# A streaming encoder step on one core: the last quarter of the second feed-forward product as seven products, GpSimd's key parts in pieces, an early sigmoid

## The chip, the cores and the metric

The kernel runs on one core of one Trainium2 chip. A core has a matrix engine (TensorE, PE in the profile, with its weight loads as PEld), VectorE (DVE), ScalarE (ACT), GpSimd (POOL) and SyncE (SP), which here only issues DMAs. The engines work side by side and wait for each other through semaphores; each runs its own instructions in a fixed order. The metric is the device time of one launch in microseconds (us), as the median of several runs.

## The reference, cut to what matters

All tensors are fp32. 576 frames (512 of the prompt, 64 of the sample) go through one layer; the change touches what stands behind the two attentions.

```python
x = LN1(alpha * x + mix @ W_o)
hid = square(relu(x @ W_up))              # 1024 -> 4096
x = LN2(alpha * x + hid @ W_down)         # 4096 -> 1024
gate = sigmoid(x @ W_ple_gate + b_ple_gate)
y = x + gate * (p @ W_ple)
```

Both layer norms subtract the mean, divide by the square root of the variance plus an epsilon, and apply a gain and an offset.

## The kernel before, in words

**Layout.** Activations lie with features across the 128 partitions and the 576 tokens along the free axis. `Y` [128, 8, 576] is the residual. `A` and `B` are the token halves 0 to 287 and 288 to 575; the last stages of the kernel before use `A2` (0 to 255) and `B2` (256 to 575) instead. PE instructions keep a 128x128 weight and stream the tokens.

**A product in fp32.** Both operands are split into a high part and a low remainder, and three matmuls (high by high, high by low, low by high) are summed in PSUM (`gemm`, line 308; `quad`, line 296, does the first piece of the gate product in another order). For the weights, ACT rounds a loaded tile `wraw` to the high half of `whl` (L149), and DVE subtracts it to give the low half (L158). For the activations, `BH` and `BL` are the high and low parts behind a layer norm (L1249 by ACT, L1253 by DVE), `hidE`/`hidO` and `hA` to `hD` those of hidden columns.

**Seven products.** Most of the feed-forward work multiplies 2x2 blocks with seven block products instead of eight (`seven`, `up_pair`, `down_pair`); sums of weight blocks and of operands make up for it. Of a unit of weights, `add_seven` loads one block sum by an ordinary load and a second load that adds to it on the way (an accumulating DMA, issued by POOL, L213), and two more sums are made by DVE in place (L184, L187). The hidden columns come in eight groups of 512; groups 6 and 7, the last quarter of W_down, are done plainly by `down_last`: 192 matmuls of 256 columns for A2, then 192 of 320 for B2.

**The tail.** `LayerNorm` is written as a generator, stepped by the loop of matmuls that it runs beside (`drive`): sum over features (`add`), mean by a matmul with `onesm` (L1200), subtract, square on ACT, sum, variance (`var`, L1220), a square root on ACT (L1222), a reciprocal on DVE (L1223), a transpose by PE that spreads it (L56), then in four parts: a product on DVE (L1236), gain and offset on ACT (L1247), high part on ACT (L1249), low part on DVE (L1253). LN2 of A2 runs under `down_last(B2)`, and LN2 of B2 under the gate product of A2 (192 matmuls of 256 columns). The gate product of B2 (192 of 320) closes the kernel, with sigmoid, product and sum by ACT and DVE, and the store. `PL` is p @ W_ple, written to HBM early (`PLD`) and loaded again by one DMA of 2304 KB (L1699) for the end.

**What sets the order.** A list scheduler works from the program order with priorities (`tc.high_priority`); matmuls of `seven` are held to program order. Weight tiles go through small rings of buffers, so a load is issued when its buffer is free, and loads of one queue land in order. ACT holds one table of functions at a time: an `ACT_TABLE_LOAD` goes ahead of the first function from another one. `early` is a square root of a constant, placed ahead of LN1 so that the table is there in time (L1662).

## Time and profile before

| what | value |
|---|---|
| median of 3 runs | 764.45 us (764.35 to 764.53) |
| the profiled execution, its own time | 764.96 us |
| its span in the trace | 763.2 us |
| PE busy | 751.1 us (98% of the span), 5679 matmuls |
| DVE busy | 570.3 us (75%) |
| ACT busy | 472.6 us (62%) |
| POOL busy | 118.0 us (15%) |
| the chain that ended last | PE 78%, DVE 13%, ACT 7% |

The span is the trace's length from the first to the last instruction; some 1.8 us of the execution's own time lie around it. Busy shares are means over the whole span, so a stage is read from a view of its own stretch. A time of the chain or the timeline counts from the start of the span.

### The profile page before, as it was taken

How to read it: one execution, taken by the hardware profiler on the slowest of the kernel's cores; microseconds unless marked ns; L12 is line 12 of the kernel's file. 1: busy time of each engine (PE TensorE's matmuls, PEld its weight loads, DVE VectorE, ACT ScalarE, POOL GpSimd, SP SyncE). 2: the span in 40 equal slices, each digit the busy share in tenths (PEclk: the TensorE clock that was granted, in tenths of full speed). 3: DMA queues.
4: the chain of work that ended last, by engine and by line, in shares of the span. 5: the costliest groups of instructions: out<-in, count | busy, mean ns of one | idle time of the engine just before them, and what ended most of it. 6: DMA issues, size and time to landing. Idle time of an engine off the chain costs nothing.

```text
span 763.2 us, 14659 instructions
## 1 busy us (share of the span) xinstructions
PE 751.1 (98%) x5679; PEld 731.1 (96%) x5679; DVE 570.3 (75%) x1119; ACT 472.6 (62%) x931; POOL 118.0 (15%) x162
## 2 busy tenths in 40 slices
PE   9999999999999999999999999999999999999997
PEld 7999998999999999999999999999999999999997
DVE  6788888888777766779787589866897766757643
ACT  6589777888667535788643577435763466525351
POOL 7100434445341000100000000000000000011000
PEclk9999999999999999999999999999999999999999
DMA  8538344254223325352447667667657564730001
GB/s 286 169 69 151 128 131 127 71 174 161 82 94 92 97 74 168 125 160 84 112 111 188 157 143 178 148 156 189 160 134 186 159 144 147 287 116 28 28 29 69
DMA packets 38198, 101.35 MB, mean 133 GB/s; under 512 B 6000, under 2 KB 10224, under 8 KB 38000
## 3 DMA queue, kind: packets, MB, share of 16 engines
q1 hardware_dynamic: 34384, 87.61, 37.4%
q0 software_dynamic: 3456, 12.58, 10.1%
q8 instruction: 44, 0.72, 0.4%
q10 hardware_dynamic: 288, 0.22, 0.1%
q14 instruction: 26, 0.21, 0.1%
HBM read 85.26 MB, written 9.54 MB: 124 GB/s over the span
## 4 chain that ended last, share of the span: by engine, by line
PE 78%; DVE 13%; ACT 7%; issue 2%; DVEq 0%; ACTq 0%
PE g L308 39%; PE m L308 14%; PE n L308 13%; PE g L296 2%; DVE dbias L713 2%; PE T L56 2%; ACT xr L791 2%; DVE whl L158 2%; DVE m L711 1%; PE V L978 1%; ACT whl L149 1%; PE m L472 1%; DVE sP L911 1%; PE m L486 1%; PE S L903 1%
## 5 line engine op out<-in xcount | busy, mean ns | idle before, releaser
L149 ACT CAST whl<-wraw 128x1024 fp32r<-128x1024 f32 (+2 forms) x190 | 154.9, 828 | 83.8 <-PE g L308 49.8
L158 DVE TENSOR_TENSOR whl<-wraw,whl 128x1024 fp32r<-128x1024 f32 (+2 forms) x158 | 157.9, 1009 | 54.0 <-ACT whl L149 53.4
L308 PE MATMUL m<-AH,whl 128*128 128x288 f32 x736 | 176.6, 307 | 0.0
L308 PE MATMUL g<-BH,whl 128*128 128x288 f32 (+2 forms) x680 | 143.3, 298 | 0.0
L308 PEld LDWEIGHTS m<-AH,whl 128*128 128x128 f32 x736 | 126.4, 188 | 1.7 <-issue 1.0
L308 PEld LDWEIGHTS g<-BH,whl 128*128 128x128 f32 x680 | 111.1, 188 | 1.3
L308 PE MATMUL m<-AL,whl 128*128 128x288 f32 x368 | 108.7, 295 | 0.0
L308 PE MATMUL g<-BL,whl 128*128 128x288 f32 (+2 forms) x340 | 100.6, 296 | 0.3 <-DVE BL L1253 0.3
L308 PEld LDWEIGHTS m<-AL,whl 128*128 128x128 f32 x368 | 69.5, 189 | 0.7
L213 POOL DMA_DIRECT2D wraw<-in_w_dram x24 | 20.7, 864 | 287.2 <-DMA wraw<-in_w_dram 173.3
L308 PEld LDWEIGHTS g<-BL,whl 128*128 128x128 f32 x340 | 64.0, 188 | 0.9 <-DVE BL L1253 0.7
L158 POOL TENSOR_TENSOR whl<-wraw,whl 128x256 fp32r<-128x256 f32 x64 | 50.6, 821 | 84.2 <-ACT whl L149 70.0
L916 ACT ACTIVATE sP<-sP,st 128x128 f32<-128x128 f32 (+4 forms) x72 | 39.5, 550 | 36.1 <-DVE st L911 36.0
L308 PE MATMUL m<-BH,whl 128*128 128x288 f32 x192 | 42.9, 302 | 0.0
L308 PE MATMUL g<-s,whl 128*128 128x288 f32 x288 | 42.1, 295 | 0.0
L308 PE MATMUL n<-BH,whl 128*128 128x288 f32 x192 | 42.0, 294 | 0.0
L308 PEld LDWEIGHTS g<-s,whl 128*128 128x128 f32 x288 | 39.5, 188 | 0.0
L308 PEld LDWEIGHTS m<-BH,whl 128*128 128x128 f32 x192 | 32.0, 188 | 0.5 <-issue 0.3
L56 PE MATMUL T<-ident,sP 128*128 128x128 f32 (+1 forms) x176 | 31.1, 273 | 1.0 <-DVE sP L925 0.6
L308 PEld LDWEIGHTS n<-BH,whl 128*128 128x128 f32 x192 | 32.0, 188 | 0.0
L1523 ACT ACTIVATE g<-n 128x288 f32<-128x288 f32 x24 | 9.5, 395 | 35.6 <-PE n L308 35.6
L308 PE MATMUL m<-BL,whl 128*128 128x288 f32 x96 | 28.3, 294 | 0.0
(331 smaller groups left out, 1662.1 us busy)
## 6 DMA issues: line engine op xcount, KB each, us to landing
wraw<-in_w_dram SPq DMA_DIRECT2D x48, 512.0 KB, 4.0
wraw<-in_w_dram POOLq DMA_DIRECT2D x24, 512.0 KB, 5.7
wraw<-in_w_qkv_dram SPq DMA_DIRECT2D x23, 512.0 KB, 4.0
wraw<-in_w_dram SPq DMA_DIRECT2D x24, 256.0 KB, 4.2
wraw<-in_w_up_dram SPq DMA_DIRECT2D x8, 512.0 KB, 4.0
wraw<-in_w_down_dram SPq DMA_DIRECT2D x8, 512.0 KB, 4.5
wraw<-in_w_gate_dram SPq DMA_DIRECT2D x8, 512.0 KB, 4.6
wraw<-in_w_o_dram SPq DMA_DIRECT2D x8, 384.0 KB, 3.1
```

The lines of the kernel that those rows point to most:

```text
L56: PE.transpose(out, in_, ident[:n, :n])
L149: ACT.copy(self.hv[u][:, 0, c], src["tile"][:, c])
L158: eng.tensor_tensor(t[:, 1, p], src["tile"][:, p], f(t[:, 0, p]), OP.subtract)
L213: POOL.dma_start(t[:, :n], it["acc"], accum_op=OP.add)
L296: PE.matmul(ps, W(w, k, slice(0, 128)), a[:, k, sl], start=(len(terms) == 2 and n == 0), stop=False)
L308: mm = PE.matmul(ps, W(w, kw, wc), a[:, ka, cols], start=(first and i == 0), stop=(last and i == n - 1), skip_group_check=more)
L472: PE.matmul(mk[:, h, :HW], w0(part, k), a[:, k, h * HW:(h + 1) * HW], start=(k == 0 and i == 0), stop=(k == 7 and i == 2))
L486: PE.matmul(acc[b][:n[b], :304], a[:, k, b * 128:b * 128 + n[b]], ixw(part, k), start=(k == 0 and i == 0), stop=(k == 7 and i == 2))
L713: tc.keep_in_program_order(DVE.match_replace(out=s, in_to_replace=m, in_values=s, imm_value=GONE))
L791: q(lambda r=r, s=s: ACT.mul(v2(xr[r * 32:r * 32 + 32]), v[s * 32:s * 32 + 32], sc))
L916: ACT.activation(j["P"], j["P"], AF.Exp, bias=j["st"][:, 0:1], scale=-1.0, accum_out=j["st"][:, 2:3])
L1523: ACT.mul(P.e, P.o, -1.0)
```

## The change

The last quarter of W_down is done in seven block products as well. Their order is not that of `seven`: `five(L2B)` does the five products that need the weight sums, for all four pairs of output columns (240 matmuls of 288 columns; new units of weights, `add_five`), and completes half B of the residual; then `two()` does the remaining two products for half A with plain W_down (96 matmuls of 288). LN2 of B runs beside `two()`, LN2 of A beside the gate product of B. Both gate products are now of 288 columns. Matmuls of these last stages: 768 before, 720 now.

Beside it: the sums of a layer norm built with `soon` are made on DVE and not on POOL (L1A, L2B); the layer norms of the tail take their buffers from those of finished products (`Carved`); PL is loaded ahead of `five`; GpSimd's subtractions for the keys (`KL`) are made in two pieces each; `early` has a buffer of its own, and a sigmoid of a constant is issued right behind the square root of L2A; the last column is split 176/112 instead of 192/128.

```diff
+        def add_five(self, ap):
+            u = len(self.cs)
+            self.cs += [128] * 3
+            r1 = self.source(ap[:, 0:1024], acc=ap[:, 1024:2048])
+            r2 = self.source(ap[:, 2048:3072])
+            lo, hi, all2 = slice(0, 512), slice(512, 1024), slice(0, 1024)
+            def t1():
+                DVE.tensor_tensor(r2["tile"][:, lo], r2["tile"][:, lo], r1["tile"][:, lo], OP.add)
+            def t2():
+                DVE.tensor_tensor(r2["tile"][:, hi], r2["tile"][:, hi], r2["tile"][:, lo], OP.add)
+            self.split(u, r2, [lo], DVE)
+            self.split(u + 1, r1, [all2], DVE)
+            self.piece(u + 1, None, t1, r1, r2)
+            self.piece(u + 2, None, t2, r2)
+            self.split(u + 2, r2, [all2], DVE)
+            return u
...
-        for kind, n in (("P", 4 if q else 0), ("Q", 4 if q < 3 else 0)):
+        for kind, n in (("P", 4 if q else 0), ("Q", 4)):
             for x in range(n):
-                U[kind, q, x] = WT.add_seven(I["w_7"][n7])
+                U[kind, q, x] = (WT.add_five if (kind, q) == ("Q", 3) else WT.add_seven)(I["w_7"][n7])
                 n7 += 1
-    for g in range(G_DOWN, NG):
-        for c in range(4):
-            U["D", g, c] = WT.add(I["w_down"][(g - G_DOWN) * 4 + c], 256, whole=True)
+    for c in range(4):
+        U["D", c] = WT.add(I["w_down"][c], 256, whole=True)
...
-        q(lambda: eng.tensor_tensor(KL[lo, 0], k32[lo, :NP], f(QE[lo, :NP]), OP.subtract))
-        q(lambda: eng.tensor_tensor(KL[hi, 1], k32[hi, :NP], f(QO[hi, :NP]), OP.subtract))
+        cuts = (slice(0, 256), slice(256, NP)) if eng is POOL else (slice(0, NP),)
+        for r, x, t in ((lo, 0, QE), (hi, 1, QO)):
+            q(lambda r=r, x=x, t=t: [eng.tensor_tensor(KL[r, x, c], k32[r, c], f(t[r, c]), OP.subtract) for c in cuts])
...
+            self.soon, self.scaling = soon, False
+            self.eng = DVE if soon else POOL
...
-                (DVE if self.sl is A else POOL).tensor_tensor(self.s, y[:, 0:2], y[:, 2:4], OP.add)
+                self.eng.tensor_tensor(self.s, y[:, 0:2], y[:, 2:4], OP.add)
-                (DVE if j == 6 or self.sl is A else POOL).tensor_tensor(self.s, self.s, y[:, j:j + 2], OP.add)
+                (DVE if j == 6 else self.eng).tensor_tensor(self.s, self.s, y[:, j:j + 2], OP.add)
...
+            first = tc.high_priority if self.soon else ExitStack
...
-            ACT.activation(rt[:, :m], var[:, :m], AF.Sqrt, bias=epst[:, 0:1])
+            root = ACT.activation(rt[:, :m], var[:, :m], AF.Sqrt, bias=epst[:, 0:1])
+            if gi and sl is A:
+                with tc.issue_after(root.ins), tc.high_priority():
+                    ACT.activation(early[:, 0:1], epst, AF.Sigmoid, bias=epst[:, 0:1])
...
-        split("12", v)
-        later(2, lambda: tt(v, v, F[0], OP.add))
+        d = 6 if g == NG - 1 else 0
+        split("12", v, d)
+        later(2 + d, lambda: tt(v, v, F[0], OP.add))
         if g > 1:
-            split("s4", v, 2)
...
+    def five(ln):
+        tt = DVE.tensor_tensor
+        oldest = [U["Q", 3, 0]]
+        def product(u, n, ps, first=True):
+            while owed.get(ROWS[n]):
+                pop_now()
+            x = HX[ROWS[n]]
+            W = WT.quarter(u, n, oldest[0])
+            for _ in gemm(ps, W, range(4), x[0], x[1], slice(0, HW), first=first, more=not first, pin=True):
+                WT.step()
+                yield 1
+        os = {}
+        def start(c):
+            u = U["Q", 3, c]
+            o = psum_n()[:, :HW]
+            yield from product(u, "11", o)
+            os[c] = d = psM.tile([128, 2, 512], F32, name="g", tag="m", bufs=2)[:, 1, :HW]
+            with tc.high_priority():
+                ACT.copy(d, o)
+            y = Y[:, 2 * c, A]
+            later(0, lambda: tt(y, y, o, OP.add))
+        yield from start(0)
+        for c in range(4):
+            u = U["Q", 3, c]
+            y0, y1 = Y[:, 2 * c], Y[:, 2 * c + 1]
+            oldest[0] = u + 1
+            z = psB.tile([128, 2, 512], F32, name="g", tag="g", bufs=1)[:, 0, :HW]
+            yield from product(u, "t0", z)
+            later(0, lambda z=z, y0=y0: tt(y0[:, B], y0[:, B], z, OP.add))
+            later(0, lambda z=z, y1=y1: tt(y1[:, B], y1[:, B], z, OP.subtract))
+            if c < 3:
+                yield from start(c + 1)
+            d = os[c]
+            yield from product(u, "t1", d, False)
+            r = fs.tile([128, 2, 2, HW], F32, name="r", bufs=2)[:, 0, 0]
+            with tc.high_priority():
+                ACT.mul(r, d, -1.0)
+            e = psum_n()[:, :HW]
+            yield from product(u, "t3", e)
+            oldest[0] = u + 2
+            def both_halves(r=r, y1=y1):
+                y = y1.rearrange("p (a t) -> p a t", a=2)
+                tt(y, y, r[:, None, :].to_broadcast([128, 2, HW]), OP.add)
+            later(0, lambda r=r, e=e: tt(r, r, e, OP.add))
+            later(0, both_halves)
+            yield from product(u, "t2", d, False)
+            def last(d=d, y0=y0, c=c):
+                with tc.high_priority():
+                    tt(y0[:, B], y0[:, B], d, OP.add)
+                    ln.add(2 * c)
+            later(0, last)
+    def two():
+        def prepare(c):
+            m = psum_g()
+            ACT.copy(m[:, :, :HW], Y[:, 2 * c:2 * c + 2, A])
+            return m
+        nxt = prepare(0)
+        for c in range(4):
+            W = unit_w(U["D", c])
+            m = nxt
+            if c < 3:
+                nxt = prepare(c + 1)
+            for x, n in ((0, "12"), (1, "s4")):
+                for _ in gemm(m[:, x, :HW], W, range(4), HX[n][0], HX[n][1], slice(0, HW),
+                              wc=slice(x * 128, (x + 1) * 128), first=False, more=True):
+                    WT.step()
                     yield 1
+            later(0, lambda c=c, m=m: ACT.copy(Y[:, 2 * c:2 * c + 2, A], m[:, :, :HW]))
...
-    L1A = LayerNorm(A, 0, (4, 5, 2, 12))
-    L1B = LayerNorm(B, 0, (3, 8, 7, 12))
+    L1A = LayerNorm(A, 0, (4, 5, 2), True)
+    L1B = LayerNorm(B, 0, (3, 8, 7))
     L1 = both(L1A, L1B)
     drive(wo2(A, L1A, 3), 8, None, 0)
-    early = lnp[0].tile([128, 4], F32, name="ln_r", bufs=2)
+    early = base.tile([128, 1], F32, name="early")
     ACT.activation(early[:, 0:1], epst, AF.Sqrt, bias=epst[:, 0:1])
...
-        if g < G_DOWN:
+        if g < NG - 2:
             todo += [down_pair(g + 1, c) for c in range(4)]
     drive(seven(todo), len(todo) * 14, None, 0)
+    PL = base.tile([128, 8, NT], F32, name="PL", tag="AH")
+    SP.dma_start(PL.rearrange("p j t -> p (j t)"), PLD)
+    lnp[0] = Carved()
+    L2B = LayerNorm(B, 2, (5, 9, 3), True)
+    L2A = LayerNorm(A, 2, (5, 8, 2))
+    drive(five(L2B), 40, None, 0)
     WT.lag = 1
+    drive(two(), 16, iter(L2B), 32, False)
+    while not L2B.scaling:
+        L2B.pump()
     pS.close()
     fe = ctx.enter_context(tc.tile_pool(name="fe", bufs=1))
     WT.ring(fe, 0, 5, "e")
     lnp[0] = fe
-    PL = base.tile([128, 8, NT], F32, name="PL", tag="AH")
-    SP.dma_start(PL.rearrange("p j t -> p (j t)"), PLD)
-    L2A = LayerNorm(A2, 2, (4, 8, 2, 0))
-    L2B = LayerNorm(B2, 2, (5, 8, 2, 0))
-    drive(down_last(A2, L2A), 32, None, 0)
-    drive(down_last(B2, L2B), 32, iter(L2A), 28)
+    for j in (0, 2, 4, 6):
+        L2A.add(j)
...
-        for _ in gemm(m[:, :320], W, range(8), BH, BL, B2):
+        for _ in gemm(m[:, :HW], W, range(8), BH, BL, A):
...
-        ps = [slice(0, 192), slice(192, 320)] if c == 7 else [slice(0, 320)]
+        ps = [slice(0, 176), slice(176, HW)] if c == 7 else [A]
...
-    drive(seq(gate(lo, A2, L2A), gate(hi, A2, L2A)), 32, iter(L2B), 25)
-    drive(seq(gate(lo, B2, L2B), gate((4, 5), B2, L2B), gate_one(6), gate_one(7)), 32, None, 0)
+    drive(seq(gate(lo, B, L2B), gate(hi, B, L2B)), 32, iter(L2A), 25)
+    drive(seq(gate(lo, A, L2A), gate((4, 5), A, L2A), gate_one(6), gate_one(7)), 32, None, 0)
```

Where the instructions stand now is set by the scheduler. Lines below are those of the program that each row comes from; the change shifts them, L308 to L328, L296 to L316, L1220 to L1243, L1249 to L1274, L1222 to L1245.

PE, from the variance of the first LN2 to the first gate matmuls, before (LN2 of A2; `n<-onesm` is the variance, `n<-ident` the transposes, `g<-BH` the gate):

```order
L1220 MATMUL n<-onesm,ln_s 128x1 x2
L308 MATMUL g<-hidO,whl 128x320 x6
L308 MATMUL g<-hidE,whl 128x320 x6
L56 MATMUL n<-ident,ln_r 128x128 x2
L308 MATMUL g<-hidE,whl 128x320 x18
L308 MATMUL g<-hidO,whl 128x320 x48
L296 MATMUL g<-BH,whl 128x256 x16
```

The same place now (LN2 of B; `g<-hB` and `g<-hD` are `two()`):

```order
L328 MATMUL g<-hB,whl 128x288 x12
L328 MATMUL g<-hD,whl 128x288 x12
L1243 MATMUL n<-onesm,lnA 128x1 x3
L56 MATMUL n<-ident,lnB 128x128 x3
L316 MATMUL g<-BH,whl 128x288 x16
L316 MATMUL g<-BL,whl 128x288 x8
```

Between the variance and the transposes stood 12 matmuls and now stand none; between the transposes and the gate stood 66 and now stand none.

ACT over the same stretch now (`lnB` is the square root, `Y<-Y,gb` gain and offset, `BH` the high part; the casts L149 make gate weights):

```order
L1245 ACTIVATE lnB_7948<-n_8412,epst_62 128x3
L149 CAST whl_8506<-wraw_8365 128x1024
L1272 ACTIVATE Y_2777<-Y_2777,gb_63 128x288 x2
L149 CAST whl_8514<-wraw_8401 128x1024
L1274 CAST BH_1145<-Y_2777 128x2x288
```

A weight cast stands between gain and offset and the first `BH`, as one did before.

PE, the first nine products of `five`, which are new (`whl_7993` and `whl_8033` belong to the second pair of output columns, `whl_8065` to the third):

```order
L328 MATMUL n_7949<-hA_7428,whl_7853 128x288 x12
L328 MATMUL g_7968<-hA_7428,whl_7902 128x288 x12
L328 MATMUL n_7986<-hA_7428,whl_7964 128x288 x12
L328 MATMUL g_7966<-hC_7789,whl_7956 128x288 x12
L328 MATMUL n_8026<-hC_7789,whl_7902 128x288 x12
L328 MATMUL g_7966<-hB_7672,whl_7956 128x288 x12
L328 MATMUL g_8058<-hA_7428,whl_7993 128x288 x12
L328 MATMUL n_8074<-hA_7428,whl_8065 128x288 x12
L328 MATMUL g_8004<-hC_7789,whl_8033 128x288 x12
```

ACT there (`wraw_7928` is the third pair's load with the accumulating DMA):

```order
L149 CAST whl_8065<-wraw_7983 128x512
L149 CAST whl_8082<-wraw_7928 128x1024
L149 CAST whl_8033<-wraw_7843 128x1024
L1679 COPY g_8093<-n_8074 128x288
L1698 ACTIVATE r_8112<-g_8004 128x288
```

`whl_8082`, wanted by the twelfth product, stands ahead of `whl_8033`, wanted by the ninth.

SP's loads around PL before (`in_w_down` are the units of `down_last`):

```order
L211 DMA wraw<-in_w_down_dram 128x1024 x3
L1699 DMA PL<-PLD 128x4608
L211 DMA wraw<-in_w_down_dram 128x1024 x3
L211 DMA wraw<-in_w_gate_dram 128x1024 x8
```

And now (`in_w` are the units of `five`):

```order
L231 DMA wraw<-in_w_dram 128x1024 x2
L1777 DMA PL<-PLD 128x4608
L231 DMA wraw<-in_w_dram 128x1024 x4
L231 DMA wraw<-in_w_down_dram 128x1024 x3
L231 DMA wraw<-in_w_gate_dram 128x1024
L231 DMA wraw<-in_w_down_dram 128x1024
```

PL now stands between the loads of the second pair and those of the third, whose first is `wraw_7928`.

ACT at the first layer norm, before:

```order
L149 CAST whl<-wraw 128x512 x4
L1662 ACT_TABLE_LOAD
L1662 ACTIVATE ln_r<-epst 128x1
L149 CAST whl<-wraw 128x1024
L1281 COPY g<-Y 128x2x288
```

And now, where `early` stands fourth in ACT's whole program and the load has come to the square root of LN1's half A:

```order
L149 CAST whl<-wraw 128x1024
L1344 COPY PL<-g 128x576
L1245 ACT_TABLE_LOAD
L1245 ACTIVATE ln_r<-n,epst 128x3
L1344 COPY PL<-g 128x576
L1229 ACTIVATE ln_s<-Y 128x576
```

The table load has moved from some twenty rows ahead of that square root to the row ahead of it; there are six loads in the program, and there were five.

More of the change, by code (lines that the diff above doesn't have):

```diff
@@ L389, in tile_hybrid_step @@
     NG = 8
-    G_DOWN = 6
     for g in range(2):
@@ L1203, in steps @@
             for j in range(0, 8, 2):
-                DVE.tensor_tensor(y[:, j:j + 2], y[:, j:j + 2], mb, OP.subtract)
-                if j == 0:
-                    ACT.activation(ss, y[:, 0:2], AF.Square)
-                else:
-                    sq = lnp[0].tile([128, 2, 320], F32, name="ln_sq", bufs=2)[:, :, :w]
-                    ACT.activation(sq, y[:, j:j + 2], AF.Square)
-                    DVE.tensor_tensor(ss, ss, sq, OP.add)
-                if j == 6:
-                    self.fold(ss)
+                with (tc.high_priority if gi and self.soon else ExitStack)():
+                    DVE.tensor_tensor(y[:, j:j + 2], y[:, j:j + 2], mb, OP.subtract)
+                    if j == 0:
+                        ACT.activation(ss, y[:, 0:2], AF.Square)
+                    else:
+                        sq = lnp[0].tile([128, 2, HW], F32, name="ln_sq", bufs=2)
+                        ACT.activation(sq, y[:, j:j + 2], AF.Square)
+                        DVE.tensor_tensor(ss, ss, sq, OP.add)
+                    if j == 6:
+                        self.fold(ss)
                 yield 1
@@ L1230, in steps @@
             rb2 = rb[:, None, :].to_broadcast([128, 2, w])
-            first = tc.high_priority if sl.start == 0 else ExitStack
+            self.scaling = True
             def scale(j):
@@ L1372, in split @@
             later(d, low)
-        if g >= G_DOWN:
-            oh, ol = [hid[g][:, x, b, (A, B)[t]] for x in range(2)]
-            later(0, lambda: ACT.copy(oh, v))
-            later(0, lambda: DVE.tensor_tensor(ol, v, f(oh), OP.subtract))
-            return
         F = [HX["f"][:, x, b] for x in range(2)]
@@ L1563, in target @@
         def target(t):
-            return HX["f"][:, t, b] if g < G_DOWN and g % 2 == 0 else P.r[:, t]
+            return HX["f"][:, t, b] if g % 2 == 0 else P.r[:, t]
         def t0():
@@ L1625, in down_pair, with __init__, tile @@
         return P
-    def down_last(sl, ln):
-        w = sl.stop - sl.start
-        g0 = NG - 2
-        ms = {}
-        n = 0
-        todo = [(j, 0) for j in (0, 2, 4)] + [(0, 1), (2, 1), (6, 0), (4, 1), (6, 1)]
-        for j, part in todo:
-            if part == 0:
-                ms[j] = psum_g()
-            m = ms[j]
-            g = g0 + part
-            W = unit_w(U["D", g, j // 2], U["D", g0, 0] if sl is A2 else U["D", g0, j // 2])
-            for x in range(2):
-                for _ in gemm(m[:, x, :w], W, range(4), hid[g][:, 0], hid[g][:, 1], sl,
-                              wc=slice(x * 128, (x + 1) * 128), first=(part == 0), last=(part == 1)):
-                    n += 1
-                    WT.step(sl is B2 or n > 18)
-                    yield 1
-            if part == 1:
-                def ev(j=j, m=m):
-                    y = Y[:, j:j + 2, sl]
-                    DVE.tensor_tensor(y, y, m[:, :, :w], OP.add)
-                    ln.add(j)
-                later(0, ev)
+    class Carved:
+        def __init__(self):
+            a = fs.tile([128, 2, 4, HW], F32, name="lnA", tag="hF").rearrange("p a b c -> p (a b) c")
+            b = fs.tile([128, 2, 4, HW], F32, name="lnB", tag="s3").rearrange("p a b c -> p (a b) c")
+            self.parts = {"ln_s": [a[:, 0:2]], "ln_sq": [a[:, 2:4], a[:, 4:6]],
+                          "ln_r": [b[:, 0, 0:4], b[:, 0, 8:12]]}
+        def tile(self, shape, dt, name, tag=None, bufs=1):
+            p = self.parts[name]
+            p.append(p.pop(0))
+            return p[-1]
@@ L1779, in _laid_out @@
     out["w_up"] = units(w_up[:, :1024], 128)
-    out["w_down"] = np.concatenate([units(w_down[g * 512:g * 512 + 512], 256) for g in (6, 7)])
+    out["w_down"] = units(w_down[3584:], 256)
     def seven(w):
@@ L1790, in _laid_out @@
         s7 += [seven(w_up[:, n:n + 256]) for n in range(q * 1024, q * 1024 + 1024, 256) if q]
-        s7 += [seven(w_down[q * 1024:q * 1024 + 1024, n:n + 256]) for n in range(0, 1024, 256) if q < 3]
+        s7 += [seven(w_down[q * 1024:q * 1024 + 1024, n:n + 256]) for n in range(0, 1024, 256)]
     out["w_7"] = np.stack(s7)
```

27 lines of the change are left out of this document (11 added, 16 removed).

## The prediction

> **What bounds the kernel now.** The page first, for the busy shares and the chain.
>
> ```profile
> span 763.2 us, 14659 instructions
> PE 751.1 (98%) x5679; PEld 731.1 (96%) x5679; DVE 570.3 (75%) x1119; ACT 472.6 (62%) x931; POOL 118.0 (15%) x162
> PE 78%; DVE 13%; ACT 7%; issue 2%; DVEq 0%; ACTq 0%
> ```
>
> PE works all the time, so fewer matmuls are time won, as long as PE is not left waiting. Next the waits of PE from 640 us to the end, which hold one row, and the chain over that stretch.
>
> ```profile
> PE g L308 <- DVE BL L1253: 0.3, 1, 0.3
> ```
> ```profile
> 649.66 1.59 PE n L308 x12
> ...
> 680.67 12.33 PE g L308 x84
> ...
> 705.11 2.88 PE g L296 x24
> ...
> 758.43 0.03 ACTq L1740
> ```
> ```profile
> 652.85 8.64 PE L308 MATMUL g<-hidE,whl 128*128 128x256 f32 x72
> ```
>
> The reader is to see two things. The tail before waits 0.3 us in all, so no wait there can be removed for more than that. And the rates: a matmul of 288 columns takes 1.59/12 = 0.1325 us, of 320 12.33/84 = 0.1468, of 256 2.88/24 = 0.120. T0, where the last quarter of W_down begins, is 652.85 us (the timeline's row). The last matmul ends at 758.43.
>
> **The change, part by part.** The sum is against the profiled execution, 764.96 us, which stands 0.5 above the median of 764.45.
>
> *PE's work.* Before: 384 x 0.120 + 384 x 0.1468 = 102.45 us for down and gate. Now 720 x 0.1325 = 95.4. That is **-7.05**. Three variance matmuls and transposes in place of two for the first LN2 half: some +0.25.
>
> *DVE in `five`.* A window ahead of the tail, where seven products run, and the prices.
>
> ```profile
> 580.00:640.00 60.00, 60.00 (x451) 59.65 (x450) 40.34 (x57) 32.98 (x50) 3.44 (x4) 1.00 0.64 158
> ```
> ```profile
> L158 DVE TENSOR_TENSOR whl<-wraw,whl 128x1024 fp32r<-128x1024 f32 x17 | 20.8, 1224 | 9.8 <-ACT whl L149 9.5
> L1603 DVE TENSOR_TENSOR Y<-Y,g 128x288 f32<-128x288 f32 x10 | 4.3, 450 | 5.0 <-PE g L308 5.0
> L184 DVE TENSOR_TENSOR wraw<-wraw 128x512 f32<-128x512 f32 x5 | 3.5, 693 | 0.2
> L187 DVE TENSOR_TENSOR wraw<-wraw 128x512 f32<-128x512 f32 x5 | 3.5, 691 | 0.2
> L158 DVE TENSOR_TENSOR whl<-wraw,whl 128x512 fp32r<-128x512 f32 x5 | 3.4, 685 | 0.0
> ```
>
> There DVE (third busy figure) works 40.34 of 60 us, two thirds. In `five`, each pair of output columns asks of DVE two weight lows of 1024 and one of 512 (2 x 1.22 + 0.69), two weight sums (2 x 0.69), five updates of 288 columns (5 x 0.45), the update of both halves and the layer norm's sum (2 x 0.75 by the 576-column row below): 8.3 us. PE's 60 matmuls take 7.95. DVE goes from two thirds to full, and it begins with the operands of group 7 still to make. What such a handover costs is to be seen at the one before:
>
> ```profile
> 564.38 1.45 PE L308 MATMUL n<-hC,whl 128*128 128x288 f32 x7
> ...
> 566.23 0.93 PE L308 MATMUL n<-hC,whl 128*128 128x288 f32 x5 [0.40 <-DVE hC L1369]
> ...
> 567.00 1.76 PE L308 MATMUL g<-hB,whl 128*128 128x288 f32 x12
> ```
>
> From 564.38 to 567.00 are 2.62 us for 12 matmuls that take 1.59: 1.0 us lost to an operand's low part. At full DVE I expect waits of that size, or a little less, at three of `five`'s twenty products: where a new pair's weight low comes behind the updates. The overrun alone is 4 x 0.35 = 1.4 us, three such waits 3.1; I take **+2.8**. Bounds: 0 (instructions overlap, so that DVE's real pitch is under these durations) and 5.
>
> *The weights of the second and third pair.* SP's queue, ACT and the accumulating DMA:
>
> ```profile
> 649.69 0.33 SPq L1699 DMA_DIRECT2D PL<-PLD  x1
> 650.74 8.15 SPq L211 DMA_DIRECT2D wraw<-in_w_down_dram  x3
> ```
> ```profile
> 660.90 1.05 ACT L149 CAST whl<-wraw 128x1024 fp32r<-128x1024 f32 x1 [2.68 <-DMA wraw<-in_w_down_dram]
> ```
> ```profile
> wraw<-in_w_dram POOLq DMA_DIRECT2D x24, 512.0 KB, 5.7
> ```
>
> The load behind PL is issued at 650.74 and lands at 660.9, T0 + 8.05, because PL's 2304 KB are ahead of it. Now that place is the third pair's first load. The accumulating DMA goes on top: T0 + 13.75. ACT's cast of it (1.05) stands ahead of the cast that the second pair's `t1` product wants: 14.8, then 15.85, then DVE's low at 17.1. PE reaches that product after 96 matmuls, T0 + 12.7, with two waits of the kind above about 14. It waits 1.85 for the high part, and its third matmul 1.0 more for the low: **+2.9**. Bounds: 0, if the load is issued two loads earlier and misses PL, and 4.5.
>
> *LN2 of B with no cover.* Between the variance and the gate's first matmul PE has the transposes and nothing else; the chain is bare. Prices:
>
> ```profile
> 318.50 0.30 PEld L1200 LDWEIGHTS n<-ln_s,onesm 128*128 128x128 f32 x2 [0.24 <-DVE ln_s L1179]
> ...
> 692.84 0.50 PE L1220 MATMUL n<-onesm,ln_s 128*128 128x1 f32 x4
> ...
> 693.38 0.26 ACT L1222 ACTIVATE ln_r<-n,epst 128x2 f32<-128x2 f32 x1 [1.93 <-PE n L1220]
> 693.67 0.17 DVE L1223 RECIPROCAL ln_r<-ln_r 128x2 f32<-128x2 f32 x1 [0.97 <-ACT ln_r L1222]
> ...
> 700.48 0.61 ACT L1249 CAST BH<-Y 128x512 fp32r<-128x512 f32 x1
> ```
> ```profile
> L1236 DVE TENSOR_TENSOR Y<-Y,n 128x576 f32<-128x576 f32 x8 | 5.5, 750 | 1.1 <-PE n L56 1.1
> L149 ACT CAST whl<-wraw 128x1024 fp32r<-128x1024 f32 x96 | 100.3, 1048 | 55.9 <-PE g L308 49.8 <-DMA wraw<-in_w_down_dram 3.1 <-DMA wraw<-in_w_gate_dram 1.2
> L1247 ACT ACTIVATE Y<-Y,gb 128x288 f32<-128x288 f32 x16 | 9.5, 629 | 1.9 <-DVE Y L1236 1.9
> L1249 ACT CAST BH<-Y 128x576 fp32r<-128x576 f32 x8 | 5.4, 675 | 0.1
> ```
>
> Root 0.26 and reciprocal 0.17, then product 0.75, two gains 1.26, the weight cast between them and the high part 1.05, high part 0.68: 4.2 us, of which 3.75 in one piece. Some 0.1 of handoffs, 0.3 for the low part as in the row of PE's waits, 0.3 for the variance's own sums, which come from DVE as at 318.50: **+4.9**. Bounds: 3.2 (the cast slips out of the way) and 8 (the same chain before, when it had cover: 692.84 + 0.50 to 700.48 + 0.61). Nothing is queued on PE that could run in it; what waits behind is the whole gate product.
>
> *The granted clock.* What idling does to PE, at the end, and what a start at the low rate looks like:
>
> ```profile
> 760.00:761.00 1.00, 0.00 (x0) 0.00 (x0) 0.00 (x0) 0.00 (x0) 0.00 (x0) 1.00 0.29 94
> 761.00:762.00 1.00, 0.00 (x0) 0.00 (x0) 0.00 (x0) 0.00 (x0) 0.00 (x0) 0.65 0.24 69
> 762.00:763.00 1.00, 0.00 (x0) 0.00 (x0) 0.00 (x0) 0.00 (x0) 0.00 (x0) 0.50 0.02 8
> ```
> ```profile
> 1.53 4.02 PE L352 MATMUL V<-warm 128*128 128x512 bf16 x9 [1.53 <-DVE warm L324]
> ```
>
> The figure behind the busy times falls to half about 761.3, 2.9 us behind the last matmul. The first nine matmuls of 512 columns take 0.447 us each, where 0.1325/288 a column would be 0.236: about 4 us at half rate. The 3.75 us piece is longer than 2.9, so the gate should start at half rate and lose up to half of 4.0: **+2.0**, bounds 0 and 2.0. By the Trainium skill ("TensorE: Matmul & The Clock Gate", section "What's actually happening") the clock halves after an idle window of about 3.4 us and comes back after as much work: a piece of 3.75 may or may not hold a whole window, and the price would be 1.7 instead of 2.0. The trace's fall after 2.9 us speaks for the earlier drop.
>
> *LN1 and the start.* ACT at LN1's half A, PE's first matmul behind it, and a table load:
>
> ```profile
> 319.86 0.26 ACT L1222 ACTIVATE ln_r<-n,epst 128x3 f32<-128x3 f32 x1 [0.94 <-PE n L1220]
> ...
> 327.87 1.98 PE L296 MATMUL g<-BH,whl 128*128 128x288 f32 x13
> ```
> ```profile
> 728.60 1.28 ACT L1722
> ```
>
> The load now stands directly ahead of that root. ACT was idle 0.94 us there, which hides as much of the 1.28; 0.34 remain. Behind it there is no slack, since PE took up `BH` as soon as it was there. I take **+0.5** for 0.34 and the second-order delay, bounds -0.5 (its sums on DVE come earlier) and +1.3. The start has one more table load, 1.28 us on an ACT that is 62% busy: **+0.2**, bounds 0 and 1.3. By the Trainium skill ("ScalarE: Activation LUTs", "What ACT_TABLE_LOAD costs") a switch costs 2.66 us with its drain, which would add 1.4 to each of the two; the row has 1.28 and no drain of that length.
>
> *At nothing:* GpSimd's key parts in pieces (POOL is busy 15%), the early sigmoid and the sums on POOL for L2A (192 gate matmuls, 25.4 us, cover both; PE waited 0.3 there before). If that cover failed, L2A's chain would show a wait of the 1.28 us load. The shorter last piece: **-0.05**.
>
> *Sum:* -7.05 + 0.25 + 2.8 + 2.9 + 4.9 + 2.0 + 0.5 + 0.2 - 0.05 = +6.45, so 771.4 profiled, **770.9** as a median.
>
> **The rivals.**
>
> *`five` fed in time (the other side).* Place: DVE and the third pair's weights in `five`. If instructions overlap enough and the load misses PL, 5.7 us go; with the bare chain at the durations alone, 4.2 + 0.1, its longest piece nearer the clock's limit and the clock kept, the sum is -7.05 + 0.25 + 4.3 + 0.65 = -1.85: 762.6 as a median. It decides at the waits of `five` and the gap together: below 6.1 us the change is even, below 4.6 faster by over 0.2%, which is about what a measurement here can tell from no change. For it: DVE's share is an average that a pitch 10% shorter would bring under PE's. Against it: the handover above, with a DVE at two thirds, already lost a microsecond.
>
> *The clock stays up.* Only the last mechanism fails: -2.0, 768.9. For it: the transposes fall into the gap, and the piece behind them is only 0.85 us over the limit seen.
>
> *The change doesn't do what it says.* POOL still makes two sums for L2A, and the early root is at the start. Were L2A's sums on DVE and the root where it was, 0.5 to 0.7 us would be won: 770.2.
>
> *A longer gap.* Its chain as loose as before, 8 us: 774.
>
> **How the numbers follow.** Forecast, with its clock drop and waits of this size, 0.42; clock kept or the edits at LN1 and the start free, 768 to 770, 0.19; longer gap or waits, over 773, 0.12; `five` fed in time 0.27, of which 0.15 faster by over 0.2%, 0.09 within it, 0.03 slower by little. Faster 0.15, same 0.09, slower 0.76. The range leaves out the faster end and the worst bounds together, 2 in 10: 764.0 to 775.0.
>
> **What would show it.** PE's waits in the profile of the changed kernel: rows on L158's `whl` and on L149's `whl` in the 40 us behind the last up product, 5 to 6 us in all; one wait on `BH` at the gate's start, 3.5 to 5 us, with a granted clock below 1.00 in the microseconds behind it; ACT's square root of LN1 with a table load ahead. I am wrong if PE's idle time there is under 7 us, if DVE's busy share in `five` is below nine tenths, or if the gate starts under other work.

## The result, and the profile after

| kernel | median | range | ratio to before | 95% interval |
|---|---|---|---|---|
| before | 764.45 us | 764.35 to 764.53 | 1 | |
| after | 772.68 us | 771.92 to 774.17 | 1.0111 | 1.0099 to 1.0123 |

The change makes the kernel 1.1% slower, 8.2 us. The profiled execution is the slowest of the four, 774.17 us with a span of 772.5, so sums against it are 1.5 us too high for the median.

PE's waits from 640 us to the end, where the kernel before had one row of 0.3 us (each row: waiting line, what it waited for, us in total, times, longest):

```profile
PE g L316 <- ACT BH L1274: 3.7, 1, 3.7
PE g L328 <- DVE whl L158: 2.0, 3, 1.1
PE g L328 <- ACT whl L149: 1.5, 1, 1.5
PE n L56 <- DVE lnB L1249: 0.7, 1, 0.7
PE n L328 <- DVE whl L158: 0.4, 1, 0.4
```

Two groups are to be seen: weights (`whl`) in the five products, and the layer norm's chain (`lnB`, `BH`) ahead of the gate. PE's timeline of the stretch, with T0 at 655.65:

```profile
665.81 1.60 PE L328 MATMUL g<-hA,whl 128*128 128x288 f32 x10 [0.15 <-DVE whl L158]
...
668.10 1.60 PE L328 MATMUL n<-hA,whl 128*128 128x288 f32 x10 [0.43 <-DVE whl L158]
671.18 0.53 PE L328 MATMUL g<-hC,whl 128*128 128x288 f32 x2 [1.48 <-ACT whl L149]
672.44 2.77 PE L328 MATMUL g<-hC,whl 128*128 128x288 f32 x10 [0.73 <-DVE whl L158]
675.00 2.06 PE L328 MATMUL n<-hC,whl 128*128 128x288 f32 x12
676.90 1.76 PE L328 MATMUL g<-hB,whl 128*128 128x288 f32 x12
...
689.64 1.60 PE L328 MATMUL g<-hC,whl 128*128 128x288 f32 x10 [1.14 <-DVE whl L158]
...
707.90 0.83 PE L1243 MATMUL n<-onesm,lnA 128*128 128x1 f32 x6
709.38 0.51 PE L56 MATMUL n<-ident,lnB 128*128 128x128 f32 x3 [0.66 <-DVE lnB L1249]
713.59 3.73 PE L316 MATMUL g<-BH,whl 128*128 128x288 f32 x16 [3.69 <-ACT BH L1274]
```

A product of twelve matmuls that runs freely takes 1.6 us from start to start. The one at 672.44 took 2.56 for ten, and the one at 675.00 1.90: PE worked slowly there without a wait. The windows say why (us, then busy time with instructions of PE, PEld, DVE, ACT, POOL, then the granted clock):

```profile
668.82:672.23 3.41, 1.42 (x9) 0.94 (x7) 1.07 (x1) 2.29 (x3) 0.87 (x1) 1.00 0.23 94
672.23:675.64 3.41, 3.20 (x13) 3.20 (x14) 3.41 (x7) 0.34 (x1) 0.00 (x0) 0.50 0.86 136
709.78:713.19 3.41, 0.12 (x2) 0.00 (x0) 3.03 (x5) 3.26 (x5) 2.81 (x2) 1.00 0.27 102
713.19:716.60 3.41, 3.01 (x12) 3.01 (x13) 3.41 (x5) 3.41 (x7) 0.00 (x0) 0.50 0.00 0
```

While PE had work left the clock fell to half twice, for 3.41 us each: behind the wait in the five products and behind the one at the gate. Half of 3.41 us is 1.7, the most that such a fall can cost. By the starts in the timeline the first cost 1.5 us (2.56 us for ten matmuls that take 1.33, then 1.90 for twelve that take 1.60) and the second 1.4 (3.57 us for sixteen that take 2.13).

Where the first wait came from is on the chain of waits, in order of time:

```profile
653.58 9.27 DMA wraw<-in_w_dram
...
663.52 5.54 DMA wraw<-in_w_dram
...
669.13 2.00 ACT whl L149 x2
...
671.16 1.24 DVE whl L158
```

The third pair's first load needed 9.27 us behind PL, the accumulating DMA 5.54 on top, and then two casts in the order that the program had shown, the wanted one second.

### The profile page after: what moved, and what is told of

The parts are those of the page before. It is cut to its first block, busy times and chain, and to the rows that moved or that the text cites. A ratio compares the mean times of both kernels' runs of the same rounds, so it can differ in the third digit from the quotient of the medians.

```text
span 772.5 us, 14682 instructions
## 1 busy us (share of the span) xinstructions
PE 752.2 (97%) x5634; PEld 730.7 (95%) x5634; DVE 591.5 (77%) x1167; ACT 491.0 (64%) x963; POOL 119.9 (16%) x176
## 4 chain that ended last, share of the span: by engine, by line
PE 76%; DVE 12%; ACT 6%; DMA 4%; issue 2%; SPq 0%; ACTq 0%; DVEq 0%; POOLq 0%
PE g L328 33%; PE m L328 17%; PE n L328 13%; DMA wraw<-in_w_dram 3%; DVE whl L158 2%; PE g L316 2%; DVE dbias L731 2%; PE T L56 2%; PE V L997 2%; ACT whl L149 2%; DVE m L729 1%; ACT xr L809 1%; PE m L490 1%; PE S L922 1%; PE m L504 1%
## 5 line engine op out<-in xcount | busy, mean ns | idle before, releaser
L149 ACT CAST whl<-wraw 128x1024 fp32r<-128x1024 f32 (+2 forms) x198 | 161.4, 828 | 74.2 <-PE g L328 32.8
L158 DVE TENSOR_TENSOR whl<-wraw,whl 128x1024 fp32r<-128x1024 f32 (+2 forms) x166 | 163.9, 997 | 47.1 <-ACT whl L149 46.3
L328 PE MATMUL m<-AH,whl 128*128 128x288 f32 x736 | 176.6, 307 | 0.0
L328 PE MATMUL g<-BH,whl 128*128 128x288 f32 x680 | 143.2, 298 | 0.0
L328 PEld LDWEIGHTS m<-AH,whl 128*128 128x128 f32 x736 | 126.4, 188 | 1.9 <-issue 1.0
L328 PEld LDWEIGHTS g<-BH,whl 128*128 128x128 f32 x680 | 111.6, 189 | 1.2
L328 PE MATMUL m<-AL,whl 128*128 128x288 f32 x368 | 109.0, 296 | 0.0
L328 PE MATMUL g<-BL,whl 128*128 128x288 f32 x340 | 100.6, 296 | 0.4 <-DVE BL L1278 0.4
L233 POOL DMA_DIRECT2D wraw<-in_w_dram x28 | 24.2, 863 | 331.9 <-DMA wraw<-in_w_dram 230.1
L328 PEld LDWEIGHTS m<-AL,whl 128*128 128x128 f32 x368 | 69.6, 189 | 0.7
L328 PEld LDWEIGHTS g<-BL,whl 128*128 128x128 f32 x340 | 64.3, 189 | 0.8 <-DVE BL L1278 0.7
L328 PE MATMUL m<-BH,whl 128*128 128x288 f32 x192 | 43.0, 302 | 0.0
L328 PE MATMUL g<-s,whl 128*128 128x288 f32 x288 | 42.2, 296 | 0.0
L328 PE MATMUL n<-BH,whl 128*128 128x288 f32 x192 | 42.1, 295 | 0.0
L328 PEld LDWEIGHTS g<-s,whl 128*128 128x128 f32 x288 | 39.7, 188 | 0.0
L328 PE MATMUL g<-hB,whl 128*128 128x288 f32 x240 | 35.4, 296 | 0.0
L328 PE MATMUL g<-hC,whl 128*128 128x288 f32 x192 | 30.0, 304 | 3.3 <-DVE whl L158 1.9
L328 PEld LDWEIGHTS g<-hB,whl 128*128 128x128 f32 x240 | 33.1, 188 | 0.1
L328 PEld LDWEIGHTS m<-BH,whl 128*128 128x128 f32 x192 | 32.1, 189 | 0.5 <-issue 0.3
L328 PEld LDWEIGHTS n<-BH,whl 128*128 128x128 f32 x192 | 32.2, 189 | 0.0
```

The lines of the kernel that those rows point to most:

```text
L149: ACT.copy(self.hv[u][:, 0, c], src["tile"][:, c])
L158: eng.tensor_tensor(t[:, 1, p], src["tile"][:, p], f(t[:, 0, p]), OP.subtract)
L233: POOL.dma_start(t[:, :n], it["acc"], accum_op=OP.add)
L328: mm = PE.matmul(ps, W(w, kw, wc), a[:, ka, cols], start=(first and i == 0), stop=(last and i == n - 1), skip_group_check=more)
```

## The experiments

Each is compared with the kernel before on the same chip, and read against the changed kernel's 772.68. The interval of the changed kernel is 1.0099 to 1.0123; a run whose interval overlaps it (e2, e3, e4, e6) is not told from it by its time, and that of e5 just touches it. A trace is one execution, so a difference between two traces is less sure than one between medians.

| run | median | ratio to before, 95% interval |
|---|---|---|
| e1, PL behind | 769.33 | 1.0071 (1.0058 to 1.0083) |
| e2, fill | 773.97 | 1.0122 (1.0107 to 1.0138) |
| e3, root late | 771.99 | 1.0102 (1.0088 to 1.0116) |
| e4, keys whole | 774.58 | 1.0138 (1.0120 to 1.0155) |
| e5, gate lows | 770.68 | 1.0086 (1.0073 to 1.0099) |
| e6, sums on GpSimd | 772.94 | 1.0113 (1.0099 to 1.0127) |
| c1 = e1 + e3 + e5 | 765.70 | 1.0018 (1.0009 to 1.0027) |
| c2 = c1 + e6 + one more low | 764.14 | 0.9997 (0.9988 to 1.0006) |
| c3 = c2, LN2 A's sums on DVE | 762.28 | 0.9968 (0.9956 to 0.9981) |
| c4 = c3, other lows | 763.80 | 0.9991 (0.9982 to 1.0000) |

**e1, the reload of PL.**

```diff
-    PL = base.tile([128, 8, NT], F32, name="PL", tag="AH")
-    SP.dma_start(PL.rearrange("p j t -> p (j t)"), PLD)
     lnp[0] = Carved()
...
+    PL = base.tile([128, 8, NT], F32, name="PL", tag="AH")
+    with tc.issue_after(WT.last.ins):
+        SP.dma_start(PL.rearrange("p j t -> p (j t)"), PLD)
     for j in (0, 2, 4, 6):
         L2A.add(j)
```

> The reload of PL (2304 KB) is issued behind the last loads of gate weights instead of ahead of the third pair's weights; nothing else differs. Theory (loads): in the changed kernel the third pair's first load waited 9.3 us behind PL and the accumulating DMA landed at 669.1, so PE lost 1.48 + 0.73 us at the second pair's t1 product and fell to half clock for 3.41 us, which costs 1.7. Without PL ahead the sum lands about 5 us earlier, all of that goes and DVE, which idled 2.4 us there, gets ahead for the later wait of 1.14: 4 to 5 us faster than the changed kernel, 768. Rival (DVE bounds the five products whatever the loads do): the wait moves to other products of the same stage, 1 to 2 us faster, 771 to 772.

(`WT.last` is the last of SP's weight loads, kept by one more line.) 769.33, 3.35 us less, between the two expectations. PE's waits from 640 us on:

```profile
PE g L316 <- ACT BH L1274: 3.7, 1, 3.7
PE g L328 <- DVE whl L158: 1.3, 2, 1.1
PE n L56 <- DVE lnB L1249: 0.7, 1, 0.7
PE n L328 <- DVE whl L158: 0.4, 1, 0.4
```

The row on ACT's `whl` (1.5) and 0.7 of those on DVE's are gone, with them the half clock in the five products. The wait of 1.1 for the last pair's low part stays, so DVE did not use the time it was given. In the profiled execution the gate's half clock became longer, which took some of the gain back: it lasted 6.83 us, two stretches, the first with 1.61 us of work for PE. Whether that holds for the other four executions is not on record.

```profile
702.49:705.90 3.41, 0.87 (x7) 0.57 (x6) 2.03 (x4) 2.20 (x5) 1.72 (x2) 1.00 1.08 439
705.90:709.31 3.41, 1.61 (x7) 1.61 (x7) 3.18 (x5) 3.41 (x6) 1.09 (x1) 0.50 0.93 393
```

**e2, work for PE in the gap.**

```diff
     while not L2B.scaling:
         L2B.pump()
+    fill = psum_n()
+    for _ in range(6):
+        tc.keep_in_program_order(PE.matmul(fill[:, :HW], onesm, L2B.s[:, 0], start=True, stop=True))
```

> Six matmuls of 288 columns, whose results nobody reads, are put on PE between the transposes of LN2 B and the first gate matmul; the rest is as in the changed kernel. Theory (clock): the wait for BH stays as long, but PE is not idle, the granted clock stays at 1.00 behind it, and the 3.41 us at half rate that cost 1.7 us go: 771.0. The drop inside the five products stays. Rival (the gate starts slowly for lack of low weights and BL, and the clock record is beside the point): no change, 772.7, with the first 24 gate matmuls still taking 4.8 us.

773.97, which fits neither expectation. PE's timeline around the gate's start:

```profile
709.07 3.08 PE L1788 MATMUL n<-lnA,onesm 128*128 128x288 f32 x12
711.97 2.37 PE L316 MATMUL g<-BH,whl 128*128 128x288 f32 x16
714.17 1.22 PE L316 MATMUL g<-BL,whl 128*128 128x288 f32 x8
...
717.49 0.53 PE L316 MATMUL g<-BH,whl 128*128 128x288 f32 x2 [1.70 <-DVE whl L158]
```

The mechanism is as the theory has it: the gate's first 24 matmuls go from 711.97 to 715.23 at full rate, 3.3 us, where the changed kernel needed 4.8 (chain: 713.59 to 718.38). But the scheduler had moved a weight cast out of the chain and behind it, so `BH` came earlier and a low part came late: ACT had made its cast by 713.90, but DVE stood idle for 2.83 us, until 715.54, for a sum of GpSimd's that came first in DVE's order. The clock fell behind the new wait of 1.70 us instead. As a test of the price in us it failed; as a test of the cause it holds.

**e3, the early square root.**

```diff
-    early = base.tile([128, 1], F32, name="early")
+    early = lnp[0].tile([128, 4], F32, name="ln_r", bufs=2)
     ACT.activation(early[:, 0:1], epst, AF.Sqrt, bias=epst[:, 0:1])
+    early = base.tile([128, 1], F32, name="early")
```

> The early square root is written to the layer norm's own buffer as in the kernel before, so that it stands ahead of LN1 again and the start has one table load less; the early sigmoid keeps its own buffer. Theory (table loads): the changed kernel is 2.1 us behind at 65 us into the span and no later at LN1, so the load at the start costs about 1.5 to 2.0 us and the one at LN1 nothing: 770.7 to 771.2. Rival (the slip at the start comes from the order of the first matmuls, from the key parts in pieces or from that one execution): 772.7, no change.

771.99, 0.7 less, under half of what I expected, and with overlapping intervals. Most of the slip of 2.1 us at 65 us was that one execution's own: a mean matmul of LN1 began at 320.43 in the changed kernel's trace, at 318.53 and 318.63 in e1 and e2, which have the same start, at 318.04 here and at 318.50 in the kernel before. The traces of all runs together say more. T0 lies between 653.82 and 655.65, 654.12 in the middle, in the five traces with the changed kernel's start (the changed kernel, e1, e2, e5, e6), and between 652.50 and 653.25, 652.81 in the middle, in the five with the early root back in its place (e3, c1 to c4): 1.3 us for the two table loads together. From that mean matmul to T0 it is 335.2 to 335.3 us in the first five and 334.7 to 334.8 in the others, so the load at LN1 costs 0.5 of it.

**e4, the key parts.**

```diff
-        cuts = (slice(0, 256), slice(256, NP)) if eng is POOL else (slice(0, NP),)
+        cuts = (slice(0, NP),)
```

> GpSimd's key parts are made whole again, 512 columns at a time, as in the kernel before; the rest is as in the changed kernel. Theory: they are off the path, 772.7, within 0.3. Rival (the slip of 2 us in the first 65 us is theirs, since the pieces are more instructions on GpSimd and on the queue behind it): 770.7 to 771.2.

774.58, 1.9 above the changed kernel, 773.0 to 777.24. T0 is 654.28, inside the range of the five traces with the same start (653.82 to 655.65), so a price of the pieces ahead of T0 is not to be seen. What differs lies in the tail, which this edit doesn't touch: there the half clock at the gate lasted two stretches in the profiled execution, as in e1. The mean granted clocks of the four executions point the same way: 0.991 in the slowest (777.24) and 0.995 in the fastest (773.0). That the clock makes the whole difference was not shown.

**e5, less for DVE ahead of the gate.**

```diff
-        U["G", c] = WT.add(I["w_gate"][c], 128, whole=True)
+        U["G", c] = WT.add(I["w_gate"][c], 128, whole=True, pool_l=c in (0, 1))
```

> The low halves of the first two gate weights are made by GpSimd instead of DVE; the rest is as in the changed kernel (PL ahead of the third pair included). Theory (the gap ahead of the gate is DVE's): in the changed kernel DVE makes five lows of 1.2 us between the end of the five products and the variance, so that the variance comes when PE has run out of matmuls. With two of them on GpSimd the variance comes some 2.4 us earlier, matmuls of two() come to stand behind it and behind the transposes, the wait of 3.7 us for BH falls under 1 and the half clock there goes (1.7 us): 4 to 5 us faster than the changed kernel, 768 to 768.5; the waits in the five products stay. Rival (the chain from the square root to BH is as long as any cover that is left, or GpSimd slows DVE): 771 to 773.

770.68, 2.0 less, half of what was expected. The wait for `BH` falls to 0.2 and the clock stays up at the gate:

```profile
704.13 0.83 PE L1243 MATMUL n<-onesm,lnA 128*128 128x1 f32 x6 [0.31 <-DVE lnA L1200]
...
706.10 0.49 PE L56 MATMUL n<-ident,lnB 128*128 128x128 f32 x3
706.35 1.18 PE L328 MATMUL g<-hB,whl 128*128 128x288 f32 x7
707.37 1.76 PE L328 MATMUL g<-hD,whl 128*128 128x288 f32 x12
709.32 1.99 PE L316 MATMUL g<-BH,whl 128*128 128x288 f32 x13 [0.20 <-ACT BH L1274]
...
713.66 0.66 PE L316 MATMUL g<-BH,whl 128*128 128x288 f32 x3 [1.57 <-DVE whl L158]
```

Matmuls of `two()` now stand behind the variance and the transposes. But 1.57 us of a new wait for a gate weight's low part came, and 0.9 at the mean. In the same trace DVE's instructions beside GpSimd's work took longer: `BL` 1.95 us and that low part 2.43, where alone they take 0.75 and 1.22. That is the rival's clause that GpSimd slows DVE, and c2 and c3 come back to it.

**e6, the sums of LN2 B.**

```diff
-            self.eng = DVE if soon else POOL
+            self.eng = DVE if soon and not gi else POOL
```

> The first two sums of LN2 B over the features are made by GpSimd as in the kernel before (three instructions of 576 columns off DVE in the five products, 0.75 us each); the rest is as in the changed kernel. Theory (DVE is full in the five products): the wait of 1.14 us for a weight's low part at 688 goes, the others stay since loads set them: 771.5. Rival (DVE is not what is short there): 772.7, unchanged.

772.94, not told from the changed kernel. The wait at 688 (1.14) went, as the theory had it, and a wait of 0.75 for the mean's sum came. The waits behind PL (1.5 and 0.7) and at the gate (3.7) are as they were. A net 0.4 us of waits is less than the times can show, so this run neither proves nor refutes that DVE is short there; it shows that a microsecond taken from DVE in the five products comes back in part at the layer norm behind them.

**c1, the three together** (e1, e3 and e5, no other edit).

> PL behind the gate weights, the early square root ahead of LN1, and two gate weights' lows on GpSimd, together. Theory: the three costs add up, since each has its own place: 3.4 for the loads as measured, 0.7 for the table load as measured, 4 to 5 for the gap with its clock: 764 to 765, about the kernel before, with no half clock before the end. What is left of the 7 us of saved PE work is spent on waits of about 2.2 us in the five products, 1 at the gate and some in between: then 762 to 763. I take 763.5. Rival (one cost hides another, as when the chain at LN2 becomes late for lack of loads): 766 to 768.

765.70. The parts alone took off 3.35, 0.7 and 2.0, 6.05 in all; together they took off 7.0, so no sign is seen of one hiding another. In the profiled execution no half clock is left before the end. The three slowest of the eleven executions (766.41 to 766.52) have a mean granted clock of 0.997, the others 0.998 or more, so those three look to have one. It misses the 763.5; the new waits of e5 are still there (1.6 for a gate weight's low part, 1.0 at the mean).

**c2, more off DVE** (c1, the edit of e6, and `pool_l=c in (3,)` for the plain weights of W_down).

> As the combination of the three, and two more things off DVE: the sums of LN2 B and the low half of the last plain weight of W_down go to GpSimd. Theory: the remaining wait of 1.3 us in the five products goes, 762; faster than the kernel before. Rival (GpSimd, now with four times the work on data in the tail, slows DVE or is late itself): no faster than the combination of three.

764.14: 1.6 less than c1, and no different from the kernel before. DVE's and GpSimd's rows at the gate's start, from the timeline of all engines:

```profile
702.54 1.43 POOL L1193 TENSOR_TENSOR ln_s<-Y 128x576 f32<-128x576 f32 x1 [3.45 <-PE g L328]
...
702.98 1.60 DVE L1278 TENSOR_TENSOR BL<-Y,BH 128x576 fp32r<-128x576 f32 x1
...
704.04 1.84 POOL L1195 TENSOR_TENSOR ln_s<-ln_s,Y 128x576 f32<-128x576 f32 x1
...
704.50 2.46 DVE L158 TENSOR_TENSOR whl<-wraw,whl 128x1024 fp32r<-128x1024 f32 x1
```

Beside GpSimd's two sums a low part took 2.46 us and `BL` 1.60, twice their usual 1.22 and 0.75, just where PE waited 1.5 for that low part.

**c3, no sums on GpSimd at the gate's start.**

```diff
-            self.eng = DVE if soon and not gi else POOL
+            self.eng = POOL if gi and sl.start else DVE if soon or gi else POOL
```

> As the combination of five, but the first two sums of LN2 A over the features are made by DVE instead of GpSimd; those fall at the start of the gate product of B. In the combination of five GpSimd's two sums lay from 702.5 to 705.9 us, and in just that stretch DVE's low part BL took 1.60 us instead of 0.75 and a weight's low 2.46 instead of 1.22, and PE waited 1.5 us for that low. Theory (GpSimd's work on data holds DVE up): those two rows come back to 0.75 and 1.22, the wait of 1.5 shrinks to under 0.5, and the kernel takes about 762.8 to 763.3, faster than the kernel before by more than 0.1%. Rival (DVE's long rows are an effect of the clock or of the order, and two more instructions on DVE cost what they take): 764.1 to 765.

The line taken out is c2's. 762.28, 1.9 less than c2, and 0.32% (0.19% to 0.44%) faster than the kernel before: the version that beats both. DVE's rows for `BL` and the low part from 701 to 706 us (mean ns behind the busy us), and PE's waits from 640 on:

```profile
L1278 DVE TENSOR_TENSOR BL<-Y,BH 128x576 fp32r<-128x576 f32 x2 | 1.5, 755 | 0.0
L158 DVE TENSOR_TENSOR whl<-wraw,whl 128x1024 fp32r<-128x1024 f32 x1 | 1.2, 1218 | 0.0
```
```profile
PE n L1222 <- DVE lnA L1200: 0.8, 1, 0.8
PE g L316 <- ACT BH L1274: 0.6, 1, 0.6
PE n L1243 <- DVE lnA L1200: 0.5, 1, 0.5
PE n L328 <- DVE whl L158: 0.4, 1, 0.4
PE g L328 <- DVE whl L158: 0.2, 1, 0.2
```

The wait for the low part is gone, with two more instructions on DVE than c2 had, and both rows are back at 0.755 and 1.22 us: the theory holds and the rival falls. 2.5 us of waits are left.

**c4, GpSimd's lows moved ahead** (`pool_l` for the plain weights 2 and 3 and the gate weight 0).

> As the run with LN2 A's sums on DVE, but GpSimd makes the low halves of the last two plain weights of W_down and of one gate weight, instead of one and two: the same amount of GpSimd work, moved some microseconds ahead, away from the layer norm. Theory (GpSimd's work on data holds DVE up while they overlap): the sums of LN2 B, which took 1.62 us for two and 0.87 for the fold beside GpSimd, are quicker, the mean's and the variance's waits shrink, another 0.5 to 1 us: 762.3. Rival (the gate's first weights then are late again on DVE): 763.5 to 765, with the wait back on a gate weight's low part.

763.80 (762.55 to 764.61): the rival in time, but not in place. In the trace the mean's wait shrank from 0.8 to 0.4, and the variance's grew from 0.5 to 1.5, since a gate weight's low part was back on DVE in the layer norm. The theory's sums were not quicker: GpSimd's lows ran from 683.65 to 695.3, still over the layer norm, and the two sums that took 1.62 us in c3, in a pause of GpSimd's, took 2.37 here. The profiled execution is the fastest of the eleven. The five above 764 have a mean granted clock of 0.996 or 0.997, the six below 763.81 one of 0.998 or 0.999, so a part of the median's loss looks to be the clock's.

## Why the prediction was right, point by point

The prediction was 770.9 with a range of 764.0 to 775.0; 772.68 is 1.8 above it and inside. The mechanisms it named are there. That the sum came so near is in part luck, as the sum below shows.

- **PE's work, -7.05: near.** Outside the waits the trace's matmuls of 288 columns start 0.133 us apart, not 0.1325, which over 720 of them is 0.4 us less saved. c3, which keeps all the 48 matmuls saved and 2.5 us of waits in the tail, is 2.2 us faster than before.
- **DVE in `five`, +2.8: right in kind, 2.3 measured.** The waits for a low part at a product of the second, third and fourth pair are 0.15 + 0.43 + 1.14 us by the timeline; by the starts, with what is lost around each wait, 0.4 + 0.6 + 1.3. Their mean is under the 1.0 us of the handover that the prediction took, and they are three, as it said. DVE was full where nothing else held it:

```profile
656.00:668.00 12.00, 11.52 (x85) 11.06 (x83) 11.96 (x22) 6.40 (x12) 0.86 (x1) 1.00 0.76 254
668.00:672.00 4.00, 2.13 (x12) 1.66 (x12) 1.56 (x3) 2.29 (x3) 0.74 (x1) 1.00 0.40 140
655.65:694.27 38.62, 34.69 (x242) 33.53 (x241) 33.49 (x53) 18.38 (x29) 1.73 (x2) 0.96 0.63 196
```

  Over all twenty products (the last row) DVE's share is 0.87, since it stood idle while the loads behind PL were late. That is under the nine tenths that the prediction gave as a sign of being wrong; the sign was set without its own wait for the loads.
- **The weights behind PL, +2.9: right.** 1.48 + 0.73 us of waits, 2.7 by the starts. e1 removes them and the clock's fall by moving one DMA, so the cause is shown.
- **LN2 of B with no cover, +4.9: right.** 0.66 + 3.69 us of waits, and 0.28 between `two()` and the variance, 4.6. The 0.3 for `BL` did not come: PE's waits from 640 us on have no row for it. e5 shows that it was DVE's weight lows that kept the variance to the end of `two()`: with two of them elsewhere the scheduler put the variance ahead of 28 matmuls.
- **The granted clock, +2.0: the term that was mis-sized.** The prediction gave it to the gate alone. It fell there, for 3.41 us, which cost 1.4, and once more in the five products, which cost 1.5. There the prediction had 1.85 and 1.0 us of waits close together and did not ask the same question of them. Two falls are 3.0 instead of 2.0.
- **LN1 and the start, +0.7: right at LN1, too small at the start.** The load at LN1 costs the 0.5 that the prediction gave it. The two together cost 1.3 at T0 by the traces, so the start costs some 0.8 where the prediction had 0.2; in the medians e3 is worth 0.7, which its interval does not tell from nothing. The bound of -0.5 had no ground: L1A's sums were on DVE in the kernel before too (`self.sl is A` in the diff's old lines).
- **At nothing:** no price of GpSimd's pieces is to be seen (e4). The sums of L2A on GpSimd made PE wait nowhere in the changed kernel, where they lay beside subtractions that read PSUM; in c2, where they lay beside `BL` and a low part, they cost the 1.9 us that c3 won back. The early sigmoid wasn't tried alone.
- **The sum.** The terms as measured, with the 0.7 left as it was, make -7.05 + 0.25 + 2.3 + 2.7 + 4.6 + 3.0 + 0.7 - 0.05 = +6.45, just what was predicted: the second fall of the clock and the smaller waits cancel by luck. The measured 8.2 is 1.75 above that. From T0 to the end of the last matmul (655.65 to 767.86 against 652.85 to 758.43) the profiled execution is 6.6 longer, where these terms give 5.75; 0.4 of the rest is the rate of 0.133. Ahead of T0 the traces have 1.3 in place of 0.7. What is left, some 0.75 us in the median, is not assigned to a place.
- **The rivals.** "The clock stays up" fell. "A longer gap" didn't come. "`five` fed in time" is what c1 to c3 make of the change, but its condition, waits and gap of less than 4.6 us for a gain of over 0.2%, was too generous: c1 with 4.6 is 0.2% slower, c2 with 4.0 is even, and only c3 with 2.5 is 0.3% faster. By the prediction's sum c3 should have won some 4.3 us and won 2.2, so 2 us or more in each of these three stand in no row of PE's waits; the rate above is 0.4 of them, and the rest is open.

On the clock the Trainium skill ("TensorE: Matmul & The Clock Gate", section "What's actually happening") has windows of 3.4 us, and the traces agree: in all of them the stretches at half rate that ended before the kernel did are 3.41 us or twice that. It speaks of an idle window; here a window in which PE was busy for 1.42 of 3.41 us was enough.

## What to carry to other kernels

Saved matmuls are worth what the engines that feed them leave of it: count the instructions of DVE and ACT for each matmul of the new stage, and look for the stage where the ratio jumps. A large reload in a queue of weights is to be put behind the last load that somebody waits for, and a serial chain needs matmuls that stand behind its first step in PE's own order. Where PE waits for one and a half microseconds or more, in one piece or in two that are close, ask whether the clock falls as well: here 1.48 and 0.73 together brought a fall that cost 1.5 us, 1.70 alone in e2 brought one too, and 1.57 in e5 did not. Work moved to GpSimd is free only where DVE's instructions beside it don't wait for it.
